# One more convolution block from VectorE to TensorE in a two-layer hybrid decoder on one core

## The chip, the cores and the metric

The kernel runs on one core of a Trainium2 chip. The metric is the time of one execution in microseconds (us), as the device reports it. Five engines work side by side: TensorE (PE in the profile; PEld is its weight loads), VectorE (DVE), ScalarE (ACT), GpSimd (POOL) and SyncE (SP), whose queue starts the DMA transfers. Each engine takes its instructions in the order in which they stand in its queue, and where one waits, all behind it wait too.

## The reference

Two layers over 1040 positions (16 meta tokens and 1024 inputs) of 1024 features, all in float32. In each layer one projection of the normalized input feeds two branches: differential attention with four heads, and a convolution over 512 channels. The branches are joined, projected by `w_out` and added to the input; a SwiGLU feed-forward part of width 2816 follows. The convolution branch, which the change touches, is:

```python
def conformer_conv(u, conv_w, conv_b, ln_g, ln_b):
    a, gate = jnp.split(u, 2, axis=-1)
    z = a * jax.nn.sigmoid(gate)
    z = lax.conv_general_dilated(
        z, conv_w[:, None, :], window_strides=(1,), padding=((CONV_WIDTH - 1, 0),),
        dimension_numbers=('NWC', 'WIO', 'NWC'), feature_group_count=CONV_CH)
    z = z + conv_b
    z = layer_norm(z, ln_g, ln_b)
    return jax.nn.silu(z)
```

`CONV_WIDTH` is 31, and each channel has its own 31 taps: position t of a channel is a weighted sum of positions t-30 to t of the same channel. The layer norm goes over all 512 channels, so it starts when every channel is done.

## The kernel before

Features lie on the 128 partitions and positions along the free dimension, so that the 512 convolution channels are four blocks of 128 channels by 1040 positions. Float32 products are done as three products of split numbers: operands are split into a high and a low part (`split`, for weights by ScalarE and VectorE, lines 222 to 226), and `mm3` issues the three matmuls (line 272).

A layer begins with the projections of the heads. `weave` runs a head's attention and, by turns, a "filler" generator with work for TensorE; a ratio and the numbers that the generators yield say how far the filler runs ahead. During the fourth head the filler is `glus((1, 2))`, that is, `glu` for blocks 1 and 2: the two projections of a block in three chunks of 272, 384 and 384 positions, the sigmoid, and the product z (lines 552 to 580). After it come block 3's `glu`, the convolution of blocks 2 and 3, the norm `conv_norm` (line 636 takes its mean on TensorE), the output projection, and the feed-forward part (line 901).

A block's convolution is done in one of two ways, by the table `DVEJ`:

- `conv_dve`, for blocks 0 and 1: VectorE makes a sum y in a "big" buffer by one scaled copy (line 588) and 30 multiply-adds over the whole row (line 590, one per tap, "tap" below). They wait in a list, and a few are put between other instructions at a time. A copy on ScalarE (line 592) then brings y into the layout that the norm wants and writes it over z.
- `conv`, for blocks 2 and 3: z is stored in eight phases (position 8n + s goes to place s, n). Line 599 clears the padding columns of a gathered copy xf, and eight DMAs (line 601) put 16 channels by 8 phases on the 128 partitions for each of eight groups. For a group a 128x640 weight table `cw` is made from a small table `ct` (line 610; two `cw` buffers; for block 1 of layer 0 GpSimd makes them, else VectorE), and five matmuls of 130 or 128 columns (line 617) add up all 31 taps of 16 channels for all positions. ScalarE empties the result after every three groups (line 623), DMAs scatter it back (line 625), and line 627 adds the bias. The results lie in PSUM tiles `sc`, of which there are three, shared with the attention scores.

Attention works in blocks of 128 queries: scores (lines 455 and 456, into `sc`), their evacuation (460), row sums, the difference of the two softmaxes (471), transposes (483 and 492) and the product with the values (503). The big buffers (names S) are a pool of 15, so a new one waits until the work on a former one of the same place is done. Within this order the program's scheduler sets the order of each engine's queue before the run.

Of the kernel before, what the change touches and what calls it, by code (L numbers as in the profile page):

```python
# [43 lines left out]
PRODS = ("a11", "s3", "s2", "s1", "a12", "a22", "s4")  # L44
OCN = (0, 4, 1, 5, 2, 6, 3, 7)
RA = 2.0
DVEJ = (0, 1)
BGSTEP = 2300.0
AHEAD = 1
CB = 2  # L50
# [35 lines left out]
def build(tc, xT, w_in, w_out, w_gu, w_down, params, lams, ctab, consts, tabs, outT):  # L86
# [14 lines left out]
    def nm(s):  # L101
        uid[0] += 1
        return f"{s}{uid[0]}"

    def big(dt=F32):
        return sp.tile([P, SW], dt, tag="S", name=nm("S"), bufs=SB)
# [11 lines left out]
    def tmp(dt=F32):  # L118
        return tp.tile([P, TW], dt, tag="T", name=nm("T"), bufs=TB)
# [18 lines left out]
    def ps(tag):  # L138
        return pp.tile([P, 512], F32, tag=tag, name=nm(tag), bufs=PS_BUFS[tag])
# [25 lines left out]
    def col(name, l, i=0, n=1):  # L165
        c = PC[name, l] if l is not None else PC[name]
        return par[:, c + i:c + i + n]
# [154 lines left out]
    def drain(*gens):  # L322
        for g in gens:
            for c in g:
                tick(c)
# [64 lines left out]
    def make_stacks(st):  # L390
        stacks = []
        for c in range(2):
            q = slice(32 * c, 32 * c + 32)
            k = slice(64 + 32 * c, 96 + 32 * c)
            three = []
            for parts in (((0, q), (1, q)), ((0, k), (0, k)), ((1, k), (1, k))):
                s = big(F32R)
                for j, (x, rows) in enumerate(parts):
                    nc.sync.dma_start(s[64 * j:64 * j + 64, :L].bitcast(F32), st[x][rows].bitcast(F32))
                three.append(s)  # L400
            stacks.append(three)
        return stacks

    def project_v(l, h, rcol, out):
        wv = fetch("in", l, 3 * h + 2)
        v0 = padded(0)
        vv = big()
        out += [v0, vv]
        def turn(vT, c0, c1):
            s0 = max(c0, META)  # L410
            if c0 == 0:
                px = ps("tr")
                T_.transpose(px[:META, :P], vT[:, 0:META], ident)
                S.activation(v0[:META, :], px[:META, :P], AF.Copy, scale=rcol[:META, 0:1])
            px = ps("tr")
            for a in range(s0, c1, P):
                T_.transpose(px[:, a - s0:a - s0 + P], vT[:, a - c0:a - c0 + P], ident)
            for a in range(s0, c1, P):
                i = 1 + (a - META) // P
                S.activation(vv[:, a - META:a - META + P], px[:, a - s0:a - s0 + P], AF.Copy,  # L420
                             scale=rcol[:, i:i + 1])

        prev = None
        for c0, c1 in CH0:
            pv = ps("pj")
            mm3(pv[:, :c1 - c0], wv, hs, c0, c1)
            vT = tmp()
            S.activation(vT[:, :c1 - c0], pv[:, :c1 - c0], AF.Copy)
            if prev:
                turn(*prev)  # L430
            prev = (vT, c0, c1)
            yield 10 * (c1 - c0) + 300
        turn(*prev)
# [119 lines left out]
    def glu(l, j, rs, out):  # L553
        z = big()
        ct = None
        if j not in DVEJ:
            ct = phase[1].tile([P, 320], F32, tag="ct", name=nm("ct"), bufs=2)
            nc.sync.dma_start(ct, ctab[l, j])
        out.append((z, ct))
        if j in DVEJ:  # L560
            ph = lambda c0, c1: z[:, c0:c1].rearrange("p (n s) -> p n s", s=S8)
        else:
            ph = lambda c0, c1: z[:, :L].rearrange("p (s n) -> p n s", s=S8)[:, c0 // S8:c1 // S8, :]
        ns = lambda t, n: t[:, :n].rearrange("p (n s) -> p n s", s=S8)
        w = fetch("in", l, 12 + 2 * j)
        for c0, c1 in CH0:
            n = c1 - c0
            pa = ps("pj")
            mm3(pa[:, :n], w, hs, c0, c1)
            tt(ph(c0, c1), ns(pa, n), ns(rs[:, c0:c1], n), ALU.mult)  # L570
            yield 10 * n
        w = fetch("in", l, 13 + 2 * j)
        for c0, c1 in CH0:
            n = c1 - c0
            pg = ps("pj")
            mm3(pg[:, :n], w, hs, c0, c1)
            t = tmp()
            tt(t[:, :n], pg[:, :n], rs[:, c0:c1], ALU.mult)
            S.activation(t[:, :n], t[:, :n], AF.Sigmoid, bias=col("bglu", l, 4 + j))
            V.scalar_tensor_tensor(ph(c0, c1), ph(c0, c1), col("bglu", l, j), ns(t, n),  # L580
                                   op0=ALU.add, op1=ALU.mult)
            yield 10 * n

    def conv_dve(l, j, z, out):

        y = big()
        cw = lambda o: col("cw", l, (CW - 1 - o) * 4 + j)
        bg.append(lambda: V.tensor_scalar(y[:, :L], z[:, :L], cw(0), col("cb", l, j), op0=ALU.mult, op1=ALU.add))
        for o in range(1, CW):
            bg.append(lambda o=o: V.scalar_tensor_tensor(y[:, o:L], z[:, :L - o], cw(o), y[:, o:L],  # L590
                                                         op0=ALU.mult, op1=ALU.add))
        bg.append(lambda: S.activation(z[:, :L].rearrange("p (s n) -> p n s", s=S8),
                                       y[:, :L].rearrange("p (n s) -> p n s", s=S8), AF.Copy))
        out[j] = z

    def conv(l, j, z, ct, out):
        xf = big()
        xv = xf.rearrange("p (g n) -> p g n", g=8)
        V.memset(xv[:, :, 0:2], 0.0)
        for g in range(8):  # L600
            nc.sync.dma_start(xv[:, g, 2:2 + NS],
                              z[16 * g:16 * g + 16, :L].rearrange("c (s n) -> c s n", s=S8))
        y = big()
        out[j] = y
        py = None
        for g in range(8):
            w = phase[1].tile([P, 5 * P], F32, tag="cw", name=nm("cw"), bufs=CB)
            wv = w[:, :].rearrange("p (d c r) -> p d c r", d=5, c=16)
            a = ct[:, 40 * g:40 * g + 40].rearrange("p (d r) -> p d r", d=5)
            (G if l == 0 and j == 1 else V).tensor_tensor(wv, a.unsqueeze(2).broadcast_to([P, 5, 16, S8]),  # L610
                            m16.unsqueeze(1).unsqueeze(3).broadcast_to([P, 5, 16, S8]), op=ALU.mult)
            if g % 3 == 0:
                py = ps("sc")
            o = (g % 3) * NS
            for d in range(5):
                a = 0 if d <= 2 else 2
                T_.matmul(py[:, o + a:o + NS], lhsT=w[:, d * P:(d + 1) * P],
                          rhs=xv[:, g, 2 + a - d:2 + NS - d], start=(d == 0), stop=(d == 4))
            yield 1085
            if g % 3 == 2 or g == 7:  # L620
                g0 = g - g % 3
                ysb = tmp()
                S.activation(ysb[:, :o + NS], py[:, :o + NS], AF.Copy)
                for gg in range(g0, g + 1):
                    nc.sync.dma_start(y[16 * gg:16 * gg + 16, :L].rearrange("c (r n) -> c r n", r=S8),
                                      ysb[:, (gg - g0) * NS:(gg - g0 + 1) * NS])
        S.activation(y[:, :L], y[:, :L], AF.Identity, bias=col("cb", l, j))
        yield 0
# [53 lines left out]
    for l in range(DEPTH):  # L682
# [37 lines left out]
        acats, ccats, ys, zs = [], [], [None] * 4, []  # L720
# [10 lines left out]
        def glus(js):  # L731
            for j in js:
                yield from glu(l, j, rs, zs)
                if j in DVEJ:
                    conv_dve(l, j, zs[j][0], ys)

        st, vs = [], []
        drain(project_qk(l, 0, cosr, sinr, st, pre))
        if l == 0:
# [3 lines left out]
        for h in range(NH):  # L743
            stacks = make_stacks(st)
            vs = []
            drain(project_v(l, h, rcol, vs))
            if fin:
                finalize(*fin.pop())
            st = []
            if h + 2 == NH:  # L750
                fill, ratio = chain(project_qk(l, h + 1, cosr, sinr, st), glus((0,))), RA
            elif h + 1 < NH:
                fill, ratio = project_qk(l, h + 1, cosr, sinr, st), 1.3
            else:
                fill, ratio = glus((1, 2)), 1.8
            weave(attention(l, h, stacks, *vs, nlams[l], cats, fin), fill, ratio)
            drain(fill)
        fill = glus((3,))
# [13 lines left out]
        fill = chain(wout_attn(0), wout_attn(1))  # L772
# [3 lines left out]
        fill = chain(*[wout_attn(n) for n in range(2, KD)])  # L776
# [412 lines left out]
```

## Time and profile before

| | |
|---|---|
| median of 3 runs | 2389.68 us (2385.37 to 2391.7) |
| the profiled execution's own time | 2387.03 us |
| its span in the profile | 2385.3 us |
| mean granted TensorE clock | 0.992 of full speed |
| PE busy | 2333.7 us, 98% of the span |
| PEld busy | 2140.8 us, 90% |
| DVE busy | 1670.9 us, 70% |
| ACT busy | 987.2 us, 41% |
| POOL busy | 33.8 us, 1% |

Busy time is that of instructions that compute; a busy PE need not be at its peak, since matmuls overlap and their ends are modelled. The fourth head of layer 0 with its filler runs from about 270 to 350 us of the span, that of layer 1 from about 1450 to 1530 us; the convolution of blocks 2 and 3 follows, and the feed-forward parts begin at about 505 and 1680 us. In rows of the trace, "128*128 128x384" is a matmul's weights and its moving tile, "S<-pj,S" are output and inputs by the program's names, and a bracket at a row's end gives the idle time before it and what ended it.

### The profile page before, as it was taken

To read this page: it belongs to the slowest core of one execution; us is meant where nothing else is said; L and a number is where in the kernel's file an instruction comes from. 1 tells how busy PE (TensorE), PEld (TensorE's weight loads), DVE (VectorE), ACT (ScalarE), POOL (GpSimd) and SP (SyncE) were. 2 spreads that over 40 slices of the span, in tenths; PEclk is the share of its full clock that TensorE was granted. 3 is DMA by queue.
4 is the path that set the end of the run, shared out by engine and by line. 5 is a ranking of instruction groups with operands and counts; after the bars stand their busy time and mean duration, and the time that the engine had idled before them with its cause. 6 is when DMAs were issued, how large, how long until landed. Compare 5 with 4: busy or idle time off the path is not lost.

```text
span 2385.3 us, 36659 instructions
## 1 busy us (share of the span) xinstructions
PE 2333.7 (98%) x14407; PEld 2140.8 (90%) x14407; DVE 1670.9 (70%) x3476; ACT 987.2 (41%) x2074; POOL 33.8 (1%) x29
## 2 busy tenths in 40 slices
PE   8999999999999999999999999999999999999998
PEld 7899999989999999999999999987788888888887
DVE  7676799786656657566766768997856556556566
ACT  5565462553323223233535555536523223233242
POOL 0000000000000000000000000000000000000000
PEclk9999999999999999999999999999999999999999
DMA  4332422101112121111244314221121121111212
GB/s 163 94 76 68 121 66 61 49 29 60 46 45 64 35 63 40 59 56 43 90 128 102 74 44 112 76 54 45 36 62 55 43 62 39 59 59 39 60 56 71
DMA packets 84460, 155.29 MB, mean 65 GB/s; under 512 B 10048, under 2 KB 33600, under 8 KB 84288
## 3 DMA queue, kind: packets, MB, share of 16 engines
q1 hardware_dynamic: 84288, 152.95, 22.2%
q8 instruction: 114, 1.87, 0.3%
q14 instruction: 58, 0.48, 0.1%
HBM read 114.64 MB, written 8.45 MB: 52 GB/s over the span
## 4 chain that ended last, share of the span: by engine, by line
PE 86%; DVE 9%; ACT 2%; issue 1%; POOL 1%; DMA 1%; SPq 1%; DVEq 0%; POOLq 0%; ACTq 0%
PE pj L272 26%; PE sc L901 16%; PE pj L901 10%; PE tr L901 10%; PE sc L272 10%; DVE S L590 4%; PE tr L503 3%; PE tr L272 2%; PE sc L455 2%; PE tr L492 1%; PE sc L456 1%; PE sc L199 1%; DVE S L293 1%; DVE cw L610 1%; DVE S L286 1%
## 5 line engine op out<-in xcount | busy, mean ns | idle before, releaser
L272 PE MATMUL pj<-hh,w 128*128 128x384 f32 (+1 forms) x1776 | 342.5, 327 | 0.7 <-ACT S L368 0.7
L285 ACT ACTIVATE w<-w 128x512 fp32r<-128x512 f32 x308 | 187.0, 627 | 318.5 <-DVE w L293 242.9
L286 DVE TENSOR_TENSOR w<-w,w 128x512 fp32r<-128x512 f32 x308 | 209.5, 690 | 128.9 <-PE sc L901 53.8
L272 PE MATMUL pj<-S,w 128*128 128x384 f32 (+3 forms) x1164 | 296.2, 351 | 1.5 <-ACT S L285 0.9
L272 PEld LDWEIGHTS pj<-hh,w 128*128 128x128 f32 x1776 | 285.9, 189 | 2.7 <-ACT S L368 1.0
L901 PE MATMUL sc<-S,w 128*128 128x260 f32 (+1 forms) x1188 | 286.3, 322 | 0.0
L222 ACT ACTIVATE w<-w 128x512 fp32r<-128x512 f32 (+1 forms) x204 | 117.6, 577 | 308.3 <-DMA w<-in_w_down 167.9
L272 PEld LDWEIGHTS pj<-S,w 128*128 128x128 f32 x1164 | 204.4, 188 | 22.8 <-ACT S L285 1.9
L901 PEld LDWEIGHTS sc<-S,w 128*128 128x128 f32 x1188 | 198.6, 191 | 17.7
L272 PE MATMUL sc<-m,w 128*128 128x384 f32 (+3 forms) x804 | 211.5, 346 | 0.0
L272 PE MATMUL pj<-m,w 128*128 128x384 f32 (+3 forms) x804 | 211.4, 346 | 0.0
L901 PE MATMUL sc<-hh,w 128*128 128x260 f32 (+1 forms) x594 | 192.3, 324 | 6.9 <-ACT w L285 6.9
L901 PE MATMUL sc<-hl,w 128*128 128x260 f32 (+1 forms) x594 | 190.9, 321 | 0.0
L272 PE MATMUL pj<-hl,w 128*128 128x384 f32 (+1 forms) x888 | 174.4, 327 | 0.0
L223 DVE TENSOR_TENSOR w<-w,w 128x512 fp32r<-128x512 f32 (+1 forms) x204 | 127.1, 623 | 51.7 <-ACT w L222 45.2
L901 PE MATMUL tr<-S,w 128*128 128x260 f32 (+1 forms) x594 | 157.8, 320 | 3.1 <-ACT S L802 3.1
L901 PE MATMUL tr<-hl,w 128*128 128x260 f32 (+1 forms) x594 | 158.1, 320 | 0.0
L901 PE MATMUL pj<-S,w 128*128 128x260 f32 (+1 forms) x594 | 158.1, 320 | 0.0
L901 PE MATMUL pj<-hh,w 128*128 128x260 f32 (+1 forms) x594 | 157.7, 320 | 0.0
L272 PEld LDWEIGHTS sc<-m,w 128*128 128x128 f32 x804 | 143.1, 188 | 12.7
L272 PEld LDWEIGHTS pj<-m,w 128*128 128x128 f32 x804 | 143.1, 188 | 12.6
L590 DVE SCALAR_TENSOR_TENSOR S<-S,par,S 128x1037 f32<-128x1037 f32 (+15 forms) x120 | 153.2, 1278 | 0.6
(214 smaller groups left out, 4599.4 us busy)
## 6 DMA issues: line engine op xcount, KB each, us to landing
w<-in_w_gu SPq DMA_DIRECT2D x176, 256.0 KB, 3.0
S<-ST SPq DMA_DIRECT2D x96, 260.0 KB, 5.2
w<-in_w_in SPq DMA_DIRECT2D x80, 256.0 KB, 3.2
w<-in_w_down SPq DMA_DIRECT2D x96, 192.0 KB, 2.4
w<-in_w_out SPq DMA_DIRECT2D x32, 256.0 KB, 2.8
S<-in_xT SPq DMA_DIRECT2D x8, 520.0 KB, 7.3
w<-in_w_down SPq DMA_DIRECT2D x16, 256.0 KB, 2.7
S<-in_tabs SPq DMA_DIRECT2D x4, 520.0 KB, 5.4
```

What stands on the lines that cost most here:

```text
L199: T_.matmul(pb[:, a - k0:b - k0], lhsT=ones[:n_, :], rhs=dg[:n_, a - k0:b - k0], start=True, stop=True)
L222: S.activation(hi, rw, AF.Copy)
L223: V.tensor_tensor(lo, rw, hi.bitcast(F32), op=ALU.subtract)
L272: T_.matmul(out, lhsT=w[k][wi], rhs=xs[k][xi][:, c0:c1], start=(q == 0 and k == 0), stop=(q == 2 and k == n - 1))
L285: S.activation(hi, src, AF.Copy)
L286: V.tensor_tensor(lo, src, hi.bitcast(F32), op=ALU.subtract)
L293: V.tensor_tensor(o, a, b, op=op)
L455: T_.matmul(pc[:sz, :n], lhsT=qs[:, qa:qb], rhs=kk[:, k0:k1], start=True, stop=False)
L456: T_.matmul(pc[:sz, :n], lhsT=qs[:, qa:qb], rhs=kl[:, k0:k1], start=False, stop=True)
L503: T_.matmul(po[:sz, :P], lhsT=lh, rhs=rh, start=(j == 0), stop=(j == len(blocks) - 1))
L590: bg.append(lambda o=o: V.scalar_tensor_tensor(y[:, o:L], z[:, :L - o], cw(o), y[:, o:L], op0=ALU.mult, op1=ALU.add))
L901: T_.matmul(outs[c][:, :s1 - s0], lhsT=w[wi][:, k * P:(k + 1) * P], rhs=xc[q][k][xi][:, s0:s1], start=(first and p == 0 and k == 0), stop= ...
```

## The change

Block 1 leaves `DVEJ`, so that `glu` stores its z in phases and reads its `ct` table, its 30 taps, its scaled copy and its ScalarE copy go, and `conv` makes its convolution. The call stands in the filler of the fourth head, between the `glu` of block 1 and that of block 2; the ratio goes from 1.8 to 2.1. Nothing else is edited. Later lines move by 3 (line 901 becomes 904).

```diff
-DVEJ = (0, 1)
+DVEJ = (0,)
...
+        def conv1():
+            yield from conv(l, 1, *zs[1], ys)
+
...
             else:
-                fill, ratio = glus((1, 2)), 1.8
+                fill, ratio = chain(glus((1,)), conv1(), glus((2,))), 2.1
             weave(attention(l, h, stacks, *vs, nlams[l], cats, fin), fill, ratio)
```

TensorE, the fourth head of layer 0, where the last chunk of block 2's first projection ends. Before, it is followed by transposes and the next head scores:

```order
L272 MATMUL pj_3846<-hh_85,w_3520 128x384
L272 MATMUL pj_3846<-hh_86,w_3520 128x384
L483 MATMUL tr_3874<-con,p_3777 16x128
L492 MATMUL tr_3882<-con,p_3777 128x128 x4
L492 MATMUL tr_3874<-con,p_3777 128x128 x3
L455 MATMUL sc_3890<-S_3086,S_3083 128x346
L456 MATMUL sc_3890<-S_3089,S_3083 128x346
L455 MATMUL sc_3894<-S_3086,S_3083 128x346
```

and in the changed kernel by the added matmuls of block 1 (S_3712 is xf, cw the weight tables), of which three groups are shown:

```order
L272 MATMUL pj_3990<-hh_86,w_3515 128x384
L617 MATMUL sc_3725<-S_3712,cw_3723 128x130 x3
L617 MATMUL sc_3725<-S_3712,cw_3723 128x128 x2
L617 MATMUL sc_3725<-S_3712,cw_3731 128x130 x3
L617 MATMUL sc_3725<-S_3712,cw_3731 128x128 x2
L617 MATMUL sc_3725<-S_3712,cw_3748 128x130 x3
L617 MATMUL sc_3725<-S_3712,cw_3748 128x128 x2
```

Three more groups follow at once, then eight score matmuls of 456 columns, which stood between the chunks before, then the last two groups. The same order stands in layer 1.

VectorE at the same place. Before (S_3069 is y of block 0), block 0's taps are spread out among the evacuations (p<-sc) of the head scores:

```order
L590 SCALAR_TENSOR_TENSOR S_3069<-S_2721,par,S_3069 128x1013
L293 TENSOR_TENSOR S_3720<-pj_3735,S_239 128x34x8
L293 TENSOR_TENSOR S_3720<-pj_3808,S_239 128x48x8
L293 TENSOR_TENSOR S_3720<-pj_3846,S_239 128x48x8
L460 TENSOR_SCALAR p_3889<-sc_3890 128x346
```

and in the changed kernel the last of them are together, with the clearing of xf (S_3712) behind them and the evacuation of the 456-column scores after that:

```order
L590 SCALAR_TENSOR_TENSOR S_3069<-S_2721,par,S_3069 128x1013
L590 SCALAR_TENSOR_TENSOR S_3069<-S_2721,par,S_3069 128x1012
L223 TENSOR_TENSOR w_4038<-w_4035,w_4037 128x512
L590 SCALAR_TENSOR_TENSOR S_3069<-S_2721,par,S_3069 128x1011
L590 SCALAR_TENSOR_TENSOR S_3069<-S_2721,par,S_3069 128x1010
L223 TENSOR_TENSOR w_4165<-w_4162,w_4164 128x512
L599 MEMSET S_3712 128x8x2
L223 TENSOR_TENSOR w_4171<-w_4168,w_4170 128x512
L226 SCALAR_TENSOR_TENSOR w_4315<-w_4312,subs_103,w_4314 128x512
L460 TENSOR_SCALAR p_3799<-sc_3800 128x456
```

xf takes the buffer of block 0's y (S_3069). The clearing and the first gather DMA therefore wait for the ScalarE copy of line 592, which reads y after its last tap.

GpSimd, layer 0. The eight tables of block 1 stand here now, two at the kernel's start and six after the third head's norm:

```order
L535 TENSOR_TENSOR s_3217<-s_3213,mhalf 128x9
L610 TENSOR_TENSOR cw_3748<-ct_3272,con 128x640
L610 TENSOR_TENSOR cw_3761<-ct_3272,con 128x640
L610 TENSOR_TENSOR cw_3769<-ct_3272,con 128x640
L610 TENSOR_TENSOR cw_3791<-ct_3272,con 128x640
L610 TENSOR_TENSOR cw_3834<-ct_3272,con 128x640
L610 TENSOR_TENSOR cw_3843<-ct_3272,con 128x640
L535 TENSOR_TENSOR s_4233<-s_4229,mhalf 128x9
```

In layer 1 these tables stand on VectorE. In SP's queue the eight gathers stand behind six weight loads of `w_in` and ahead of the first loads of `w_out`.

## Rows read from the trace of the kernel before

**Rows 1.** The page: busy time of each engine, and shares of the last chain.
```profile
PE 2333.7 (98%) x14407; PEld 2140.8 (90%) x14407; DVE 1670.9 (70%) x3476; ACT 987.2 (41%) x2074; POOL 33.8 (1%) x29
...
PE 86%; DVE 9%; ACT 2%; issue 1%; POOL 1%; DMA 1%; SPq 1%; DVEq 0%; POOLq 0%; ACTq 0%
```

**Rows 2.** Busy us by stretch: length, PE, PEld, DVE, ACT, POOL, clock, DMA, GB/s.
```profile
340.00:420.00 80.00, 77.68 (x526) 74.37 (x525) 75.67 (x103) 27.78 (x43) 2.71 (x1) 1.00 0.28 74
...
1520.00:1600.00 80.00, 76.76 (x481) 69.69 (x480) 74.68 (x99) 29.05 (x45) 2.71 (x1) 1.00 0.27 70
```

**Rows 3.** The page's groups of instructions: the taps of blocks 0 and 1.
```profile
L590 DVE SCALAR_TENSOR_TENSOR S<-S,par,S 128x1037 f32<-128x1037 f32 (+15 forms) x120 | 153.2, 1278 | 0.6
```

**Rows 4.** Waits of PE from 340 to 440 us: total, times, longest.
```profile
PE tr L549 <- DVE o L548: 1.0, 1, 1.0
...
PE sc L636 <- ACT S L592: 0.6, 1, 0.6
```

**Rows 5.** Waits of PE from 1520 to 1640 us.
```profile
PE tr L549 <- DVE S L548: 1.7, 1, 1.7
...
PE pj L272 <- ACT S L285: 0.9, 2, 0.5
PE sc L636 <- ACT S L592: 0.8, 1, 0.8
```

**Rows 6.** Timeline of PE: start us, us, instruction; two groups of block 2.
```profile
365.43 2.39 PE L617 MATMUL sc<-S,cw 128*128 128x130 f32 x20
367.58 0.37 PE L272 MATMUL pj<-hh,w 128*128 128x272 f32 x1
```

**Rows 7.** Timeline of DVE in the fourth head of layer 0.
```profile
312.69 0.56 DVE L293 TENSOR_TENSOR T<-pj,S 128x384 f32<-128x384 f32 x1 [0.36 <-PE pj L272]
...
318.88 0.63 DVE L460 TENSOR_SCALAR_CACHE_REDUCE p<-sc 128x456 f32<-128x456 f32 x1 [0.26 <-PE sc L456]
...
320.30 1.03 DVE L471 SCALAR_TENSOR_TENSOR p<-p,s,p 128x784 f32<-128x784 f32 x1
...
322.62 1.27 DVE L590 SCALAR_TENSOR_TENSOR S<-S,par,S 128x1018 f32<-128x1018 f32 x1
...
330.67 0.68 DVE L223 TENSOR_TENSOR w<-w,w 128x512 fp32r<-128x512 f32 x1
...
332.66 2.12 DVE L293 TENSOR_TENSOR S<-pj,S 128x272 f32<-128x272 f32 x3
```

**Rows 8.** Timeline of PE over the same stretch.
```profile
312.49 0.34 PE L455 MATMUL sc<-S,S 128*128 128x392 f32 x1
...
318.26 0.37 PE L455 MATMUL sc<-S,S 128*128 128x456 f32 x1
...
319.51 0.51 PE L272 MATMUL pj<-hh,w 128*128 128x384 f32 x2
...
330.65 0.27 PE L483 MATMUL tr<-con,p 128*16 128x128 f32 x1
```

**Rows 9.** The source view of line 592: duration in ns, minimum, median, maximum.
```profile
L592 ACT ACTIVATE S<-S x4: 2098/2162/2192, 345.6 to 1595.4; 128x1040 f32<-128x1040 f32 x4
```

**Rows 10.** The source view of line 601, the gathers: from issue to landing.
```profile
DMA to landing us min/median/max: 2.4/2.5/4.5
```

**Rows 11.** Groups on DVE: the weight tables (busy, mean ns of one, idle before).
```profile
L610 DVE TENSOR_TENSOR cw<-ct,con 128x640 f32<-128x640 f32 x32 | 25.9, 818 | 0.7 <-DMA ct<-in_ctab 0.4 <-PE sc L617 0.2
```

**Rows 12.** Groups on POOL: its longest tensor operation.
```profile
L535 POOL TENSOR_TENSOR s<-s,mhalf 128x9 f32<-128x9 f32 x8 | 18.1, 2266 | 630.5 <-DVE s L533 333.4 <-DVE s L442 297.1
```

**Rows 13.** Busy time by stretch where layer 0's feed-forward part begins.
```profile
510.00:515.00 5.00, 2.29 (x12) 2.29 (x13) 5.00 (x10) 4.77 (x10) 0.00 (x0) 0.81 0.00 0
515.00:520.00 5.00, 5.00 (x38) 4.84 (x38) 3.28 (x9) 1.98 (x5) 0.00 (x0) 0.84 0.01 2
```

**Rows 14.** Waits of PE from 480 to 525 us.
```profile
PE sc L901 <- ACT w L285: 4.5, 1, 4.5
```

**Rows 15.** Waits of PE from 1640 to 1700 us.
```profile
PE tr L901 <- ACT S L802: 2.8, 1, 2.8
PE sc L901 <- ACT w L285: 2.4, 1, 2.4
```

## The prediction

> **What bounds the kernel now.** I read the page first: TensorE is busy for 98% of the span and carries 86% of the chain that ended last, VectorE 9% of it at 70% busy [rows 1]. A reader should take from this that an instruction added to TensorE's queue costs its full time unless it fills an idle moment, and that one taken from VectorE gains only where TensorE waited for it. Second, the busy time by stretch, because an average over 2385 us hides stages: where the taps run, VectorE is busy for 75.67 and 74.68 of 80 us, close to full, and TensorE still for 77.68 and 76.76 [rows 2]. So VectorE is nearly a second bound here, yet TensorE stood idle for only 2.3 + 3.2 = 5.5 us there. Third, TensorE's waits in the stretches where the taps and their copies are still near, which name what of this VectorE caused: 1.6 us in layer 0 [rows 4] and 3.4 us in layer 1 [rows 5]. Fourth, timelines of both engines at the place where the order of the changed kernel puts the new matmuls, the end of the first projection of block 2 [rows 7, 8]. There a wait would arise that the kernel before does not have.
>
> **The change part by part.**
>
> *Removed from VectorE.* 120 taps take 153.2 us [rows 3]; half of them go, 38 us in each layer. This is no gain by itself. It is worth at most what TensorE waited: 1.0 + 0.6 and 1.7 + 0.9 + 0.8 = 5.0 us [rows 4, 5], against 5.5 us of idle in the two stretches. I take **-5.0** (between 0, if other work fills VectorE's queue in front of the same waits, and -5.5).
>
> *Added to TensorE.* Two groups of five matmuls run from 365.43 to 367.58, 1.075 us a group [rows 6]. Eight groups in two layers: 16 x 1.075 = **+17.2**. TensorE has hardly any hole to take them, so all of it is on the path.
>
> *A new wait ahead of them.* By the order, the added matmuls are not woven between others: six groups stand in a row. They need xf, which takes the buffer of block 0's sum y. So the chain is: last tap of block 0, ScalarE's copy, gather DMA, first matmul, and TensorE can do nothing else meanwhile. When does each side arrive, in layer 0? VectorE, before, takes from 312.69 to 332.66 through tap 1013, that is 19.97 us [rows 7]. In the changed order the evacuation of the 456-column scores leaves this stretch (322.62 - 318.88, less the 1.03 of the subtraction that stays: 2.7) [rows 7], and so does a subtraction of 912 columns (1.03 x 912/784 = 1.2). Two more taps come in (2 x 1.27) and one more weight split (0.68) [rows 7]; 0.36 of idle at the start [rows 7] is used up by writing z of block 1 in strides, which I set as large. 19.97 - 2.7 - 1.2 + 2.5 + 0.7 = 19.3, and the last tap ends at 332.0. The copy takes 2.16 [rows 9] and the gather 2.5 from issue to landing [rows 10]: 336.7. TensorE takes from 312.49 to 330.65 to the end of the chunk [rows 8]; eight score matmuls move behind the burst (1.25 for six, so 1.7) [rows 8], and the order has one more turn of seven transposes ahead of the burst, which I set at 0.7. That gives 312.49 + 18.16 - 1.7 + 0.7 = 329.7. The wait is 336.7 - 329.7 = 7 us. Layer 1 has the same rows in the same order, so **+14**. Bounds: 0, if block 0's taps run ahead of this reckoning, and 9 a layer with the slowest landing of 4.5 in place of 2.5 [rows 10].
>
> *The clock after the wait.* The only long idle of TensorE nearby is that at the start of the feed-forward part: after 4.5 us without work [rows 14] the granted clock was 0.81 and 0.84 in the next two slices of 5 us [rows 13], part of the time at 1.2 GHz in place of 2.4. 5 x (0.19 + 0.16) = 1.75 us of full-speed work lost. A wait of 7 us should do the same: **+3.4** for two. Bounds 0 and twice that.
>
> *GpSimd's tables, layer 0.* No row shows this operation on GpSimd. On VectorE it takes 0.818 us [rows 11]; GpSimd's longest row, another operation on far fewer columns, takes 2.27 [rows 12]. I take 1.5, between the same operation and the same engine, for neither row is near. With two buffers, table 2 starts when group 0 is done, and tables 2 to 5 follow one another: 1.07 + 4 x 1.5 + 1.07 = 8.1 us in place of 6 x 1.075 = 6.45, **+1.7**. At 0.82 it is 0, at 2.27 about +5.5. Layer 1 makes them on VectorE at 0.82, faster than a group: 0. The Trainium skill ("GPSIMD Engine Reference", 3.1, the side-by-side of elementwise work) has a tensor_tensor of 2048 float32 elements take 1.96 times as long on GpSimd as on VectorE; no row here shows that pair. An estimate by it is 0.818 x 1.96 = 1.6 us, and the term would be +2.1 in place of +1.7.
>
> *Score buffers.* Right behind the burst stand four score tiles and the last two groups, with three buffers and no projection between, where before projections stood between them. I set one evacuation, 0.63 [rows 7], a layer: **+1.3** (0 to 2.5).
>
> *At nothing.* ScalarE loses a 2.16 us copy [rows 9] a layer and gains three evacuations and a bias; it is busy for 28 of 80 us there [rows 2]. The gathers and scatters on SP hold back the loads of `w_out`, which are needed only after the convolution of blocks 2 and 3; if that cover failed, a load's landing of a few us would be added once a layer. The clearing of xf holds VectorE for the copy's 2 us; behind it stand weight splits and the evacuation of scores that come after the burst, so TensorE's own wait covers it.
>
> **Sum.** 17.2 + 14 + 3.4 + 1.7 + 1.3 - 5.0 = +32.6 on the profiled execution's 2387.0, that is 2419.6. The median of the runs is 2.7 above that execution, so on its footing I say **2422**.
>
> **The rivals.**
>
> *The gather arrives in time.* If block 0's taps run some 7 us ahead of my reckoning, the wait and the clock terms fall away: 32.6 - 14 - 3.4 = +15.2, about 2405. For it: VectorE's queue is relieved, and the order already pulls the last three taps of block 0 ahead of scores behind which they stood. Against it: one buffer chains it all, and VectorE is full there [rows 2].
>
> *No slower, because VectorE's relief reaches further.* Suppose 38 us less on VectorE a layer also lets it prepare the feed-forward part early. The waits there, 4.5 + 2.8 + 2.4 = 9.7 us [rows 14, 15], and their low clock, 2 x 1.75, would go, besides the 5.0, and the gather would have to be in time: 17.2 + 1.7 - 5.0 - 9.7 - 3.5 = +0.7, about 2390. It decides if VectorE is still behind at the end of the mix stage. For it: those waits end on ScalarE's work, which needs VectorE's. Against it: from the norm on the work is a chain of its own with the same instructions in both kernels, and the taps of the changed kernel end near 332, long before this part begins. Beside it the Trainium skill ("Perfetto Trace Analysis", Identifying the Most-Contended Engine) says that matmul busy time is no measure of how near TensorE is to its limit, that VectorE is judged by its occupancy, and that the engine to relieve may change by regime; by that, relief in a stretch at 94% would pay. The trace agrees that VectorE is nearly full there, but weight loads are at 74.37 of 80 too [rows 2].
>
> *Everything at its upper bound.* Slowest landing (+4), a second low-clock stretch after each wait (+3.4), tables at 2.27 (+3.8): +43.8, about 2433.
>
> *The change does not do what it says:* the order shows a burst, not a weave. That is in the forecast already.
>
> **How the numbers follow.** The forecast 0.60, the gather in time 0.18, no slower 0.10, upper bounds 0.12. A measurement here can tell about 0.3%, 7.2 us, from no change. Of the no-slower case 0.07 lies within that and 0.03 is faster; of the gather in time 0.02 falls within it. So faster 0.03, same 0.09, slower 0.88. The range takes in the gather's case and the upper bounds: 2402 to 2437; the forecast's own is 2412 to 2429.
>
> **What the changed profile would show.** Matmuls of the convolution 480 instead of 320, at the same duration; taps 60; GpSimd with eight tables, whose mean decides that term. TensorE with one wait of 6 to 8 us in each layer, ended by the gather DMA or by what clears xf, in the fourth head near 330 and near 1510 us, and a granted clock under 0.9 in the 5 us behind it. VectorE well under 70 of 80 us after it, and the waits of lines 549 and 636 gone, while those at the start of the feed-forward part stand as before. I am wrong if that new wait is under 3 us, if conv matmuls fill idle time rather than add to it, or if the feed-forward waits shrink.

## The result, and the profile after

| | before | changed |
|---|---|---|
| median of the runs | 2389.16 us (4 runs) | 2419.39 us (4 runs, 2417.34 to 2424.14) |
| span of the profiled execution | 2385.3 us | 2415.6 us |
| mean granted TensorE clock | 0.992 | 0.991 |

The ratio is 1.0133 (95% interval 1.0121 to 1.0145), 30.2 us slower; 2422 was forecast, 2402 to 2437 the range. Where the time lies is read in the order of the prediction. The page of the changed kernel first, busy time by engine and the shares of the chain that ended last:

```profile
PE 2353.3 (97%) x14567; PEld 2159.4 (89%) x14567; DVE 1613.5 (67%) x3424; ACT 988.4 (41%) x2080; POOL 42.9 (2%) x37
...
PE 89%; DVE 6%; ACT 2%; issue 1%; POOL 1%; DMA 1%; SPq 1%; POOLq 0%; DVEq 0%; ACTq 0%
```

Beside [rows 1]: VectorE's busy time is 57 us lower and TensorE's 20 us higher, though the span has grown by 30, so TensorE has new idle time as well. The changed kernel's groups of instructions (count, busy us, mean ns, idle before and its causes) say where it lies:

```profile
L617 PE MATMUL sc<-S,cw 128*128 128x130 f32 (+1 forms) x480 | 63.5, 291 | 15.3 <-DMA S<-S 13.6 <-DVE cw L610 1.2 <-POOL cw L610 0.3
L590 DVE SCALAR_TENSOR_TENSOR S<-S,par,S 128x1039 f32<-128x1039 f32 (+29 forms) x60 | 76.9, 1281 | 0.5
```

Half the taps [rows 3] are gone, line 617 has 480 matmuls, and it waited 13.6 us for the gathers, in two waits of 7.7 and 5.9 us. The timeline of PE in layer 0, from the end of the chunk of [rows 8]:

```profile
328.04 1.57 PE L272 MATMUL pj<-hh,w 128*128 128x384 f32 x8
337.32 8.93 PE L617 MATMUL sc<-S,cw 128*128 128x130 f32 x50 [7.71 <-DMA S<-S]
346.56 1.38 PE L617 MATMUL sc<-S,cw 128*128 128x130 f32 x10 [0.31 <-POOL cw L610]
347.70 0.45 PE L455 MATMUL sc<-S,S 128*128 128x456 f32 x1
...
349.92 2.25 PE L617 MATMUL sc<-S,cw 128*128 128x130 f32 x18
```

Six groups stand in a row, and take 347.70 - 337.32 = 10.4 us where 6.45 were counted at full clock. The chain ahead of them, on DVE and then on ACT:

```profile
330.00 2.57 DVE L590 SCALAR_TENSOR_TENSOR S<-S,par,S 128x1011 f32<-128x1011 f32 x2
332.50 0.69 DVE L223 TENSOR_TENSOR w<-w,w 128x512 fp32r<-128x512 f32 x1
334.76 0.07 DVE L599 MEMSET S<- 128x16 f32 x1 [1.58 <-ACT S L592]
```

```profile
332.61 2.08 ACT L592 ACTIVATE S<-S 128x1040 f32<-128x1040 f32 x1 [3.12 <-DVE S L590]
```

Last tap at 332.5, copy to 334.7, gather landed and first matmul at 337.3: 332.0, 334.2 and 336.7 had been worked out. The busy time and the clock behind the two waits (stretch: PE, PEld, DVE, ACT, POOL, clock):

```profile
337.00:342.00 5.00, 4.68 (x22) 4.71 (x23) 0.00 (x0) 0.00 (x0) 1.29 (x1) 0.50 0.72 134
342.00:347.00 5.00, 4.58 (x33) 4.00 (x33) 1.82 (x1) 1.86 (x3) 4.59 (x4) 0.96 0.33 98
...
1530.00:1535.00 5.00, 2.69 (x12) 2.69 (x13) 0.89 (x2) 0.31 (x1) 0.00 (x0) 0.53 0.53 79
1535.00:1540.00 5.00, 5.00 (x37) 5.00 (x36) 2.97 (x4) 1.11 (x2) 0.00 (x0) 0.79 0.38 80
```

After its wait TensorE ran at its lower level, 1.2 GHz, for most of 5 us. And VectorE in the stretches of [rows 2], which now has 46 and 51 us of 80 to do instead of 75:

```profile
340.00:420.00 80.00, 78.87 (x547) 75.50 (x546) 45.79 (x97) 31.05 (x53) 9.69 (x7) 0.98 0.32 81
1520.00:1600.00 80.00, 73.30 (x495) 69.52 (x494) 50.63 (x101) 32.28 (x57) 1.80 (x1) 0.96 0.29 73
```

### The profile page after: what moved, and what is told of

Same layout as the page of the kernel before. It is cut to its first block, busy times and chain, and to the rows that moved or that the text cites. A ratio compares the mean times of both kernels' runs of the same rounds, so it can differ in the third digit from the quotient of the medians.

```text
span 2415.6 us, 37080 instructions
## 1 busy us (share of the span) xinstructions
PE 2353.3 (97%) x14567; PEld 2159.4 (89%) x14567; DVE 1613.5 (67%) x3424; ACT 988.4 (41%) x2080; POOL 42.9 (2%) x37
## 4 chain that ended last, share of the span: by engine, by line
PE 89%; DVE 6%; ACT 2%; issue 1%; POOL 1%; DMA 1%; SPq 1%; POOLq 0%; DVEq 0%; ACTq 0%
PE pj L272 27%; PE sc L904 16%; PE pj L904 10%; PE tr L904 10%; PE sc L272 10%; PE tr L503 3%; PE sc L617 2%; PE tr L272 2%; DVE S L590 2%; PE sc L455 1%; PE tr L492 1%; PE sc L456 1%; PE sc L199 1%; PE sc L636 1%; POOL s L183 1%
## 5 line engine op out<-in xcount | busy, mean ns | idle before, releaser
L272 PE MATMUL sc<-S,w 128*128 128x384 f32 (+3 forms) x444 | 147.6, 343 | 0.0
```

The lines of the kernel that those rows point to most:

```text
L272: T_.matmul(out, lhsT=w[k][wi], rhs=xs[k][xi][:, c0:c1], start=(q == 0 and k == 0), stop=(q == 2 and k == n - 1))
```

## The experiments

Twelve kernels ran, in four groups, each beside the kernel before on the same chip; each time below is against the median of before in its group, 2386.9 to 2388.5 us. On that footing the changed kernel's ratio of 1.0133 is +32. The weave's ratio stays 2.1 in every version of the changed kernel, so what its rise from 1.8 does by itself is not shown.

**Is it VectorE that TensorE waited for?** The kernel before with one block's taps left out:

```diff
-        for o in range(1, CW):
+        for o in range(1, CW if j == 0 else 1):
             bg.append(lambda o=o: V.scalar_tensor_tensor(y[:, o:L], ...
```

> The kernel before, but with block 1's 30 taps left out (only the scaled copy of line 588 is done), so VectorE has 38 us less a layer and TensorE the same work. Theory: TensorE gets back only what it waited for near the taps, 5 us, so about 2384 (2380 to 2388, ratio 0.998). Rival 1 (the relief reaches the feed-forward part as well): its waits of 10 us and the half clock behind them go too, about 2371. Rival 2 (VectorE is not waited for at all): 2389.

Measured 2383.30 us, ratio 0.9985 (0.9977 to 0.9994): 3.6 us, and by the interval 1.4 to 5.5. 76 us of VectorE's work are worth 3.6 us. That is within the 2380 to 2388 expected. At the start of the feed-forward part TensorE still waited 3.0 + 0.3 us (4.5 + 0.7 + 0.3 before) in layer 0 and 3.2 + 0.7 + 0.6 (2.8 + 2.4 before) in layer 1. Though these waits are shorter, no time is gained there: from the norm's last product (line 636) to the first scores of layer 1 TensorE takes 1248.0 - 420.7 = 827.3 us (1249.5 - 422.9 = 826.6 before), and from that of layer 1 to the end of the span 2381.5 - 1597.7 = 783.8 (2385.3 - 1602.6 = 782.7 before).

**What do the matmuls cost?** The changed kernel with block 1's matmuls doubled:

```diff
-            for d in range(5):
+            ds = list(range(5)) * (2 if j == 1 else 1)
+            for i, d in enumerate(ds):
```

> The changed kernel with every matmul of block 1's convolution issued twice, everything else the same in number. Theory (TensorE has no hole there, so the matmuls cost their full time): 16 groups of 1.075 us more, 17.2, less some 1 us in layer 0 because the tables no longer pace the burst, and with a little more of it at half clock: 2435 to 2438. Rival (part of them lie in idle time of TensorE): under 2430.

Measured 2434.56 us, ratio 1.0199 (1.0185 to 1.0213), so 0.0066 or 15.8 us above the changed kernel's 1.0133. Theory had 16.2; the two intervals together leave about 11 to 20 us, and every run (2433.3 to 2435.9) lies above the rival's 2430. By the medians the matmuls lie on the path in full.

**What does the missing buffer cost, and what do GpSimd's tables?** First each alone. A free buffer for xf:

```diff
-        xf = big()
+        xf = pair().rearrange("p a b -> p (a b)")[:, :SW] if j == 1 else big()
```

> The changed kernel, but block 1's gathered copy xf lies in one of the two pair buffers, which is free during the fourth head, so that the first gather need not wait for the last tap and the copy of block 0. Theory (the missing buffer costs the two waits of 7.7 and 5.9 us and the half clock behind each): both waits of the first L617 go, the clock stays at 1.00 there, and the time falls by 13.6 + about 4 = 17 to 19 us, to about 2401, still some 12 us above the kernel before, which is the matmuls' price less VectorE's relief. Rival 1 (VectorE is late there in any case, so another wait takes the place): it falls by less than 8 us, to 2411 or more. Rival 2 (the matmuls fill holes of TensorE once they are free to move): it falls to the kernel before or below, 2390.

Measured 2407.31 us, ratio 1.0082 (1.0068 to 1.0095), that is +20.4: the change lost 11 us of its cost, not the 17 to 19 of the theory. Both waits for the gather were gone, but in layer 0 others had come. PE's waits from 300 to 440 us in this kernel:

```profile
PE sc L455 <- DVE p L460: 2.8, 1, 2.8
PE sc L617 <- POOL cw L610: 1.8, 3, 0.8
PE sc L617 <- DVE cw L610: 0.6, 1, 0.6
```

and behind the 2.8 us the last two groups took 4.03 us (2.39 for two in [rows 6]), which is half clock again. Why VectorE was late shows in its timeline in this kernel, with POOL's beside it:

```profile
322.68 2.12 DVE L590 SCALAR_TENSOR_TENSOR S<-S,par,S 128x1017 f32<-128x1017 f32 x1
324.72 2.06 DVE L471 SCALAR_TENSOR_TENSOR p<-p,s,p 128x784 f32<-128x784 f32 x1
326.70 2.30 DVE L590 SCALAR_TENSOR_TENSOR S<-S,par,S 128x1016 f32<-128x1016 f32 x1
328.92 1.77 DVE L223 TENSOR_TENSOR w<-w,w 128x512 fp32r<-128x512 f32 x1
330.61 5.82 DVE L590 SCALAR_TENSOR_TENSOR S<-S,par,S 128x1015 f32<-128x1015 f32 x3
336.36 0.62 DVE L460 TENSOR_SCALAR_CACHE_REDUCE p<-sc 128x456 f32<-128x456 f32 x1
```

```profile
321.62 10.22 POOL L610 TENSOR_TENSOR cw<-ct,con 128x640 f32<-128x640 f32 x5 [47.26 <-PE sc L617]
332.05 2.00 POOL L610 TENSOR_TENSOR cw<-ct,con 128x640 f32<-128x640 f32 x1 [0.21 <-PE sc L617]
```

While GpSimd made tables, a tap took 2.1 to 2.3 us instead of 1.27, the subtraction of 784 columns 2.06 instead of 1.03 [rows 7], and a split 1.77 instead of 0.68 [rows 7]; and a table took 1.7 to 2.3 us, where in the changed kernel it took 1.29 with VectorE idle. The two engines hold each other up. The Trainium skill ("SBUF — State Buffer", SBUF: two separate sides) says that VectorE and GpSimd share one pair of ports, taken as an exclusive lock by a VectorE operation with two inputs in SBUF against a GpSimd operation that reads SBUF. The rows agree in kind: all four slowed operations have two such inputs.

The tables alone, in the changed kernel:

```diff
-            (G if l == 0 and j == 1 else V).tensor_tensor(wv, ...
+            V.tensor_tensor(wv, ...
```

> The changed kernel, but layer 0's eight weight tables of block 1 are made by VectorE, as in layer 1. Theory (GpSimd's 1.29 us a table paces the burst of layer 0, where a group takes 1.075): layer 0's six groups take some 1 us less than the 10.4 us of the changed kernel, and the rest of what they take over 6.45 us stays, since it is the half clock; the whole time is 0 to 2 us less. Rival (the tables are what stretches the burst from 6.45 to 10.4): it falls below 8 us.

One run: 2418.64 us, as the changed kernel. Six groups are no longer in a row here: four stand together, then two scores, then two more:

```profile
338.70 7.03 PE L617 MATMUL sc<-S,cw 128*128 128x130 f32 x40 [7.62 <-DMA S<-S]
345.49 0.45 PE L455 MATMUL sc<-S,S 128*128 128x456 f32 x1
...
346.58 2.50 PE L617 MATMUL sc<-S,cw 128*128 128x130 f32 x20 [0.43 <-DVE cw L610]
348.83 0.46 PE L455 MATMUL sc<-S,S 128*128 128x456 f32 x1
```

The first four took 345.49 - 338.70 = 6.8 us, at a granted clock of 0.50 from 337 to 342, and the other two 348.83 - 346.58 = 2.25, at full clock. Together that is 9.0 us with VectorE's tables, against 10.4 with GpSimd's and 6.45 at full clock throughout. So most of the stretching of the burst is the clock; the tables on GpSimd are some 1.4 us of it, near the 1 us of the theory, and far from the rival's "below 8".

Both together:

> The changed kernel with xf in the pair buffer (20.4 us above the kernel before) and layer 0's tables on VectorE. Theory (its tables took 1.7 to 2.3 us on GpSimd beside the taps, and TensorE waited 1.8 us for them and 2.8 us for a VectorE that ran beside them): 14 to 17 us above the kernel before, ratio 1.006 to 1.007. Rival (VectorE is late there with block 0's taps, and its own six tables of 0.82 make it later): 20 us or more, 1.0085 and up.

Measured 2399.23 us, ratio 1.0049 (1.0037 to 1.0062), +11.5: the two edits together give back 20 us, where one alone gave 11 and the other nothing. PE's waits from 280 to 440 us of this kernel, and its busy time where the burst had been:

```profile
PE sc L455 <- DVE p L463: 1.7, 1, 1.7
PE sc L617 <- DVE cw L610: 0.6, 1, 0.6
```

```profile
320.00:340.00 20.00, 20.00 (x154) 19.05 (x153) 19.49 (x35) 7.69 (x21) 0.00 (x0) 1.00 0.41 98
340.00:360.00 20.00, 20.00 (x139) 19.35 (x138) 16.39 (x39) 13.11 (x25) 0.00 (x0) 1.00 0.55 194
```

The expected 14 to 17 was too much by 3; six tables of 0.82 did not make VectorE late.

**Or is it the place?** The convolution called after both products:

```diff
-                fill, ratio = chain(glus((1,)), conv1(), glus((2,))), 2.1
+                fill, ratio = chain(glus((1, 2)), conv1()), 2.1
```

with xf from the big buffers, and from the pair:

> The changed kernel, but the convolution of block 1 is called after the products of blocks 1 and 2 instead of between them; xf still comes from the 15 big buffers. Theory (the price of the change is 17.2 for the matmuls less some 4 for VectorE's relief, and all above it is the place, where block 0's taps are not yet done): the waits of 7.7 and 5.9 us go, since block 0's copy is long done by then, and the time is 12 to 16 us above the kernel before, ratio 1.005 to 1.007. Rival (one more buffer is needed wherever it stands): a wait of line 617 for the gather of over 3 us a layer stays, and the ratio is 1.009 or more.

> As the one with the later call, but xf in the free pair buffer as well. Theory: as there, 1.005 to 1.007, since both waits are gone by the place alone. Rival (buffer and place each take a part of the wait): lower than with the place alone by over 3 us. If it comes to the kernel before or below, the reckoning that the matmuls have no idle time to fill is wrong.

Measured 2406.83 us, ratio 1.0081 (1.0068 to 1.0094), and 2406.23 us, 1.0081 (1.0067 to 1.0095): the same. The place alone takes the wait for the gather away, and the free buffer adds nothing to it. But both stay at 19 us, not the 12 to 16 expected, so the theory that all above the matmuls is the place fails; waits for tables were left in the first (2.0 for GpSimd, 0.6 and 2.6 for VectorE). Tables were tried in two ways, three buffers in place of two (in the pair), and VectorE in place of GpSimd:

```diff
+            if j == 1:
+                w = pr[:, 5 * P * (g % 3):5 * P * (g % 3 + 1)]
```

> The kernel with the later call, and with three buffers for block 1's weight tables instead of two (in a pair buffer that is free then). Its runs were 19.3 us above the kernel before, of which 17.2 are matmuls; its profile had 5.2 us of waits of line 617 for tables, from GpSimd (2.0) and VectorE (0.6 and 2.6), against 0.5 in the kernel before. Theory (these waits are what is left above the matmuls): they fall to about 1, and the time to 13 to 16 us above the kernel before, ratio 1.0055 to 1.0065. Rival (they only cover VectorE's lateness, which comes out at the next place): 18 to 20 us, ratio 1.008.

> As the one with three table buffers, with layer 0's tables on VectorE. Theory (GpSimd's 1.29 us a table no longer matters with three buffers): the same within 2 us. Rival (GpSimd still sets the pace in layer 0): 1 to 3 us faster.

> The kernel with the later call, two table buffers, and layer 0's tables on VectorE. In the kernel with the later call and three table buffers, taps that ran beside GpSimd's tables took 1.8 and 2.2 us instead of 1.28, and a wait for VectorE grew from 1.7 to 4.1 us. With tables on VectorE and three buffers the time was 12.6 us above the kernel before. Theory (the slowing of VectorE by GpSimd is what the third buffer let in, and with two buffers the early tables do the same less strongly; the waits for the third table are the smaller part): 13 to 17 us above the kernel before, ratio 1.0055 to 1.007. Rival (the third buffer is what saves): as the later call with tables on GpSimd, 19 us, 1.008.

| later call, and | ratio to before | 95% interval | us above |
|---|---|---|---|
| two buffers, GpSimd | 1.0081 | 1.0068 to 1.0094 | 19.3 |
| three buffers, GpSimd | 1.0083 | 1.0069 to 1.0096 | 19.8 |
| two buffers, VectorE | 1.0072 | 1.0058 to 1.0086 | 16.0 |
| three buffers, VectorE | 1.0054 | 1.0040 to 1.0067 | 12.6 |

The third buffer gains nothing while GpSimd makes the tables, as the rival had it and not the theory's 13 to 16, and GpSimd's part is 7 us once there is a third buffer, where at most 3 were expected. With two buffers the intervals of GpSimd's and VectorE's tables overlap widely, so neither the theory nor the rival of that run is decided. With three buffers on GpSimd three tables are made at once, early, beside the taps. The kernel with three buffers on GpSimd, on POOL:

```profile
275.54 8.62 POOL L614 TENSOR_TENSOR ST<-ct,con 128x640 f32<-128x640 f32 x3 [3.21 <-DMA S<-ST]
```

and its taps beside those of the kernel with VectorE's tables, which is the second fence:

```profile
280.81 7.10 DVE L590 SCALAR_TENSOR_TENSOR S<-S,par,S 128x1031 f32<-128x1031 f32 x4
```

```profile
279.58 5.27 DVE L590 SCALAR_TENSOR_TENSOR S<-S,par,S 128x1031 f32<-128x1031 f32 x4
```

The same four instructions take 1.8 us longer, and the first scores of the fourth head, which wait for VectorE, start after a wait of 4.1 us instead of 1.7. Behind the longer wait the granted clock is 0.57 from 290 to 295 us and 0.75 from 295 to 300, where it is 1.00 in the kernel with VectorE's tables: 3.46 us busy x 0.43 + 5 x 0.25 = 2.7 us of full-speed work. Wait and clock make 5.1 of the 7.2 us between the two; the rest is not traced. So what costs here is mostly not the pace of the tables, but what they do to VectorE just where TensorE waits for it.

**The other direction, and a search for something faster than before.** Block 2 to VectorE as well, and the same with block 1's taps on ScalarE (product) and GpSimd (addition):

```diff
-DVEJ = (0, 1)
+DVEJ = (0, 1, 2)
...
-        weave(conv(l, 2, *zs[2], ys), fill, 2.4)
...
+                    S.activation(t, z[:, :L - o], AF.Copy, scale=cw(o))
+                    G.tensor_tensor(y[:, o:L], t, y[:, o:L], op=ALU.add)
```

The first two parts of the diff are both kernels' and the third the second's. The second also keeps a list of its own for the taps of block 1 and issues one for every 4600 units of work counted (`BG2`), half as often as the other taps (`BGSTEP`, 2300).

> The opposite of the change, from the kernel before: block 2 goes to VectorE too (its call of the convolution on TensorE and its turns in the filler go). TensorE has 16 groups less, -17.2. Theory (VectorE had 4 to 11 us free of each 80 near there, about 20 from 340 to 500 us, for 38 us more a layer): the taps end after the norm is due, and TensorE waits at line 636 for some 10 to 20 us a layer: same to 20 us slower than before. Rival (what VectorE does there can wait, the taps fit): 2370.

> From the kernel before: block 1's taps go to ScalarE (product with the weight) and GpSimd (the addition), and block 2's taps to VectorE in their place, so TensorE has 16 groups less and VectorE the same number of taps, the second half of them later. If an addition of 1040 columns on GpSimd takes 1.29 x 1040/640 = 2.1 us, 30 of them end some 63 us after block 1 is ready, near 390, before the norm. Theory (idle engines take the work): 10 to 17 us faster than before, ratio 0.993 to 0.996. Rival 1 (block 2 comes late, so its 38 us of taps on VectorE hold up the norm): slower, as with three blocks on VectorE. Rival 2 (30 products of over 1.1 us on ScalarE delay the softmax and TensorE waits there): no faster than before.

Measured 2457.96 us, ratio 1.0297 (1.0283 to 1.0311), and 2483.11 us, 1.0401 (1.0387 to 1.0415). The sign of the first was right and its size was not, +70 where 0 to 20 was expected. The second, expected 10 to 17 us faster, is 96 slower, as its first rival had it and by more. ScalarE's copies of the late blocks, by its timeline in the first kernel, start at 416 and 454 us, and before the second it had idled 24 us:

```profile
415.95 2.14 ACT L592 ACTIVATE S<-S 128x1040 f32<-128x1040 f32 x1 [13.62 <-DVE S L590]
...
454.05 2.11 ACT L592 ACTIVATE S<-S 128x1040 f32<-128x1040 f32 x1 [24.03 <-DVE S L590]
```

while in the kernel before the norm's first products (line 636) start at 405.0. Its busy time shows VectorE full and what the waits did to the clock:

```profile
340.00:420.00 80.00, 64.64 (x418) 61.77 (x417) 79.01 (x99) 26.05 (x41) 2.71 (x1) 0.92 0.22 60
420.00:500.00 80.00, 57.53 (x294) 52.07 (x293) 61.84 (x97) 28.30 (x36) 1.79 (x1) 0.78 0.07 23
```

In the second kernel an addition took 2.67 us on GpSimd beside VectorE's work, not 2.1, and the last ended at 436.6 us where 390 was reckoned. Of its time from 333.9 us on, GpSimd spent 17 us waiting for ScalarE's products, which the slower issue of these taps may have caused, so the run doesn't show what the two engines could do at best. No version tried that does the whole work beats the kernel before: two blocks on each side is the best of the divisions tried.

## Why the prediction was right, by its own steps

The sum came within 2.4 us, +30.2 for +32.6, and partly by luck: the clock cost 1.5 us more than forecast and the relief gave back some 3 us more.

- **Matmuls, +17.2.** Right: doubling them added 15.8 where 16.2 was expected.
- **The wait for the gather, +14.** Right in mechanism and nearly in size: 7.7 + 5.9 = 13.6. The kernels with a free buffer, and with a later call, have no such wait. In layer 0 the chain came within 0.6 us at each step. Part of that fit is luck: VectorE's stretch lasted 20.5 us (312.0 to 332.5) where 19.3 was counted, but began 0.7 us earlier, and of the two waits one was 0.7 us too long for the 7 and the other 1.1 too short. What was not foreseen is that the wait also hid something: with it, VectorE was idle while GpSimd made six tables (POOL is busy for 4.59 of 5 us from 342 to 347, VectorE for 1.82), so that the two met only once: a split of line 226 there took 1.82 us, and the kernel before has none of that line over 0.75. Taking the wait away alone let them meet and gave back 11 us; with VectorE's tables it gave 20.
- **The clock, +3.4.** Too small by some 1.5 us; this is the step with the weakest working. Granted 0.50 and 0.96 in layer 0, 0.53 and 0.79 in layer 1: lost 4.68 x 0.50 + 5 x 0.04 and 2.69 x 0.47 + 5 x 0.21, together 4.9. The forecast's 1.75 a wait took both slices as full of work, though TensorE was busy for only 2.29 us of the first [rows 13]; counted as here the wait of 4.5 us had cost 2.29 x 0.19 + 5 x 0.16 = 1.2. The waits of 5.9 and 7.7 us cost about twice that each, and the forecast's overcount hid a part of that.
- **GpSimd's tables, +1.7.** A table took 1.29 us where VectorE was idle, less than the 1.5 taken. Of the burst's excess of 10.4 - 6.45 = 3.9 us the clock is 2.5, which leaves 1.4 for tables and the rest; the run with VectorE's tables agrees (9.0 us for six groups). The bound at 2.27 us was added up wrongly: 1.07 + 4 x 2.27 + 1.07 = 11.2, so +4.8 and not +5.5, which the forecast itself doesn't use. The Trainium skill's ratio of 1.96 ("GPSIMD Engine Reference", 3.1) had given an estimate of 1.6 us. Here the ratio is 1.29 / 0.818 [rows 11] = 1.58 without VectorE beside it, while beside VectorE's taps a table took 1.7 to 2.3 us. That second slowing is another effect, which the prediction didn't weigh; in this order it showed once.
- **Score buffers, +1.3.** The eight score matmuls of 456 columns took 2.22 us (349.92 - 347.70) in layer 0 and 2.39 in layer 1, against 8 x 0.208 = 1.66 at the pace of [rows 8]: 1.3 together. The size is right, the cause mostly open: the profile names 0.3 us in layer 0 and 0.2 in layer 1 as waits for an evacuation (line 460).
- **VectorE's relief, -5.0.** Too small. By itself it measured 3.6 in the medians (1.4 to 5.5). In the changed kernel more came back: the costs above sum to 17.2 + 13.6 + 4.9 + 1.4 + 1.3 = 38.4, the result is 30.2, so 8 us were regained, not 5. The waits of lines 549 and 636 are gone from PE's waits, as foreseen. The profiled executions bring the two closer. The first head scores (line 455), which stand long before the first tap, start at 62.0 us in the kernel before, at 64.4 in the one without block 1's taps and at 61.4 in the changed one; from there to the end of the span the three take 2323.3, 2317.1 and 2354.2 us. So the relief alone gives 6.2 us there, and the changed kernel regains 38.4 - 30.9 = 7.5. That is one execution of each, and where the last 1.3 us come from no run shows.
- **The rivals.** *The gather in time* is not what happened, but it is what the kernel with both edits is: +11.5, where the rival's sum had +15.2. *Relief that reaches the feed-forward part*: the waits there went from 9.7 to 6.1 us by the rows of lines 285 and 802 (3.0 in layer 0 and 3.1 in layer 1 are left), so I was wrong that they would stand as before. The forecast had listed their shrinking as a sign that it was wrong. It was not one, since the stretch got no shorter: from the norm's last product to the first scores of layer 1 the changed kernel takes 1265.4 - 439.0 = 826.4 us (826.6 before), and from that of layer 1 to the end 2415.6 - 1632.3 = 783.3 (782.7 before). In layer 1 other waits came in their place, as of line 199 for VectorE (4.5 us, 3.1 before) and of line 904 for lines 293 and 1033 (0.6 + 0.7). The rival's own sum leaves out the 1.3 of the score buffers, with which it gives +2.0.

## What to carry to other kernels

An engine that is 94% busy need not be one that the bound engine waits for: taking 38 us a layer from VectorE gained 3.6 us in all, and putting 8.6 a layer on TensorE cost all of it. Before moving work, follow the buffer that the moved step takes back to who frees it: here that one wait doubled the price of the change. And when one stall is removed, look at what ran in its shelter; two engines that never met in time before may meet then.

## What was not expected of the hardware

GpSimd and VectorE slowed each other to about half pace when both read SBUF: taps of 1.27 us took up to 2.30, tables of 1.29 us mostly over 2.0, and additions of 1040 columns on GpSimd 2.67 us where 2.1 was scaled from the undisturbed table. An evacuation from PSUM, with its one input there, was not slowed: in the changed kernel one of 456 columns took 0.63 us from 348.40, as in [rows 7], while GpSimd's last table ran from 348.09 in 1.29.

The division of work was also steeper than thought: 38 us more a layer on a VectorE with 4.3 + 11.3 = 16 us free from 340 to 500 us (the text before that run said some 20) cost not the difference but 35 us a layer, the matmuls saved already taken off. The late blocks hold up the norm (TensorE waited 18.0 us at line 636 in layer 0), and the granted clock was 0.78 from 420 to 500 us.
